# A hybrid SSD, mLSTM and RWKV-7 trunk on one core: its order from a recorded program and a list scheduler instead of hand-set yields, and GpSimd's tensor operations on VectorE

## The chip, the cores and the metric

The kernel runs on one core of a Trainium2 chip. A core has five engines with a queue of instructions each: TensorE (PE) for matmuls, with its weight loads shown apart (PEld), VectorE (DVE), ScalarE (ACT), GpSimd (POOL), and SyncE (SP), which here issues the DMAs. The engines meet by semaphores. The metric is the device time of one execution in microseconds, the median of several runs.

## The reference

The program is a trunk of two layers over 256 positions of width 1024, all in f32. A layer adds a half SwiGLU feed-forward network, then a mixer, then another half network; a last norm closes the trunk.

```python
for each layer:
    x += 0.5 * swiglu(rms_norm(x, n1), f1_gate_up, f1_down)     # 1024 -> 2 x 2816 -> 1024
    u = rms_norm(x, mix_norm) @ w_in                            # all head groups at once
    y = concat(ssd_mixer(u_ssd), mlstm_mixer(u_mlstm), rwkv7_mixer(u_rwkv))   # 1024 | 512 | 512
    x += y @ w_out                                              # 2048 -> 1024
    x += 0.5 * swiglu(rms_norm(x, n2), f2_gate_up, f2_down)
out = rms_norm(x, final_norm)
```

The three head groups are recurrences, computed in chunks:

```python
# SSD: causal convolution and silu, then in 2 chunks of 128, per head
y = (C B^T * decay) @ (X * dt) + (C @ state) * exp(a_cum) + X * d_skip
y = group_rms_norm(y * silu(z))
# mLSTM: q, k, v by small matmuls, exponential gates with a running maximum, 2 chunks of 128
# RWKV-7: per head of 64, a state that is decayed, corrected along a removal key and written to;
# in 4 chunks of 64, with a triangular inverse (I + A)^-1 per chunk and head, then a group norm
```

## The kernel before

**Precision and weights.** A large matmul is done in three passes of half precision each: weights and activations are split into a rounded `hi` and a rest `lo`, and PE adds hi·hi, hi·lo and lo·hi (L354 to L356 for projections, down and output weights, L571 to L573 for gate and up). The weights come from DRAM as 378 blocks of 128 x 1024 f32 (512 KB) through `load_next`; ACT copies each to `hi` (L327) and another engine subtracts to get `lo` (L328). That is DVE, but in the mixer every third block, from the sixth on, is subtracted on GpSimd: 18 blocks in each layer. There are six buffers of raw blocks and four of each half, and the split runs at most three blocks ahead of PE.

**Stages of a mixer.** The weight blocks are used in a fixed order: output gate, RWKV's r, k, v and low-rank inputs, the mLSTM input, the SSD input with its convolution, z, and then w_out. Beside these projections run the tasks: `rwkv` (L734 on), the gates of SSD and mLSTM, `mlstm`, and two parts of SSD. The RWKV task is one long chain: the shifted projections, tanh and decay (L748 to L800), the norm of the removal key with its matmul (L807, L808), the pair matrices of keys within a chunk (matmul L845, masked out of the bank at L850), and then an inverse of the triangular part. The 16 x 16 diagonal blocks of that matrix are written to DRAM by 16 DMAs (L887) and read back with each block on one partition (L889); 15 steps of two small DVE instructions solve all of them at once (L950, L952); the result goes out again (L959, L960) and comes back block by block (L969). From there small matmuls (L994) put the blocks together, and four chunks follow, each with some eight steps that depend on one another (L1044 to L1066). `put_yT` then transposes for w_out, which waits until RWKV has ended.

**What sets the order.** Program order is the order of each engine's queue. The tasks are Python generators that yield a number at each step; a `Driver` holds a clock which the main loop advances by hand-set amounts after each matmul group, and it resumes a task when the clock has passed what the task asked for. Where the main loop cannot go on without a task, `drv.until` runs tasks until a flag is set. The tasks' buffers come from one arena of 104 x 256 columns, and a task that finds no room yields. PSUM is split into four accumulator banks, three for projections and one for transposes.

Of the kernel before, what the change touches and what calls it, by code (L numbers as in the profile page):

```python
# [37 lines left out]
R_NM, R_SSD, R_DSK, R_ML, R_LNW, R_LNB, R_AL = 0, 1024, 2048, 3072, 3584, 4096, 4608  # L38
NPR = 4644
# [10 lines left out]
NRAW = 6  # L50
FIRST = ((0, 1), (2, 3))
FIRST_M = ((0, 1, 2, 3), ())
NHL = 4
YIELD = {'rwkv': 1.8, 'rwkv_norm': 2.07, 'gates': 1.8, 'mlstm': 1.8, 'ssd_a': 1.61, 'ssd_b': 1.8}
POOL_LO = 3
POOL_0 = 5
ADV = (10.5, 1.3, 1.3, 5.2, 2.6)
ARENA = 104 * 256


class Arena:


    def __init__(self, ap, n):
        self.ap, self.free, self.used = ap, [(0, n)], {}
        self.peak, self.n = 0, n

    def get(self, n):
        best = None
        for i, (o, m) in enumerate(self.free):  # L70
            if m >= n and (best is None or m < self.free[best][1]):
                best = i
        assert best is not None, (n, self.free)
        o, m = self.free.pop(best)
        if m > n:
            self.free.append((o + n, m - n))
        v = self.ap[:, o:o + n]
        self.used[id(v)] = (o, n, v)
        self.peak = max(self.peak, self.n - sum(m for _, m in self.free))
        return v  # L80

    def fits(self, n):
        return any(m >= n for _, m in self.free)

    def grab(self, n):

        while not self.fits(n):
            yield 1.0
        return self.get(n)

    def put(self, *views):
        for v in views:
            o, n, _ = self.used.pop(id(v))
            self.free.append((o, n))
            self.free.sort()
            merged = []
            for a, b in self.free:
                if merged and merged[-1][0] + merged[-1][1] == a:
                    merged[-1] = (merged[-1][0], merged[-1][1] + b)
                else:  # L100
                    merged.append((a, b))
            self.free = merged


class Driver:


    def __init__(self):
        self.t, self.tasks = 0.0, []

    def spawn(self, gen):
        self.tasks.append([self.t, gen])

    def _run(self, task):
        try:
            w = next(task[1])
        except StopIteration:
            self.tasks.remove(task)
            return
        task[0] = self.t + YIELD[task[1].__name__] * w  # L120

    def adv(self, dt):
        self.t += dt
        for task in list(self.tasks):
            if task[0] <= self.t:
                self._run(task)

    def until(self, ready):
        while not ready():
            task = min(self.tasks, key=lambda x: x[0])  # L130
            self.t = max(self.t, task[0])
            self._run(task)
# [3 lines left out]
def kernel(ctx: ExitStack, tc: tile.TileContext, x, pvec, prow, fnorm, w_gate,  # L136
                             w_in, w_out, f1_gu, f1_dn, f2_gu, f2_dn, wq, wk, wv, w_up, a_up, g_up, out):
    nc = tc.nc
    pe, act, dve, gps, sp = nc.tensor, nc.scalar, nc.vector, nc.gpsimd, nc.sync

    const = ctx.enter_context(tc.tile_pool(name="const", bufs=1))
    rawp = ctx.enter_context(tc.tile_pool(name="rawp", bufs=NRAW))
    hip = ctx.enter_context(tc.tile_pool(name="hip", bufs=NHL))
    lop = ctx.enter_context(tc.tile_pool(name="lop", bufs=NHL))
    rowp = ctx.enter_context(tc.tile_pool(name="rowp", bufs=1))
    smp = ctx.enter_context(tc.tile_pool(name="smp", bufs=4))
    ptp = ctx.enter_context(tc.tile_pool(name="ptp", bufs=2))
    dramp = ctx.enter_context(tc.tile_pool(name="dramp", bufs=2, space=bass.MemoryType.DRAM))
    ps_acc = ctx.enter_context(tc.tile_pool(name="ps_acc", bufs=4, space=PSUM))
    ps_mm = ctx.enter_context(tc.tile_pool(name="ps_mm", bufs=3, space=PSUM))  # L150
    ps_tr = ctx.enter_context(tc.tile_pool(name="ps_tr", bufs=1, space=PSUM))

    def mmb():
        return ps_mm.tile([128, 512], F32, tag="mm", name="mm")

    def trb():
        return ps_tr.tile([128, 512], F32, tag="tr", name="tr")

    def accb():
        return ps_acc.tile([128, 512], F32, tag="acc", name="acc")  # L160
# [7 lines left out]
    arena_t = const.tile([128, ARENA], F32, name="arena")  # L168
    ar = Arena(arena_t, ARENA)
    res = const.tile([128, 2, D], F32, name="res")  # L170
    hT_hi = const.tile([128, 8, T], F32R, name="hT_hi")
    hT_lo = const.tile([128, 8, T], F32R, name="hT_lo")
# [13 lines left out]
    br = const.tile([128, T], F32R, name="br")  # L186

# [5 lines left out]
    def build_consts():  # L193
        dve.tensor_copy(out=identr, in_=ident)
        dve.tensor_tensor(out=selr, in0=ident[:, 0:64], in1=ident[:, 64:128], op=ALU.add)
        mk = ar.get(256)
# [13 lines left out]
        bones = ar.get(128)  # L210
# [4 lines left out]
        ar.put(bones)  # L215
# [13 lines left out]
        dve.memset(mk, 0.0)  # L229
        dve.tensor_copy(out=br, in_=mk)  # L230
        ar.put(mk)
# [12 lines left out]


    specs = []
    on_pool = set()

    def spec_gu(w, j):
        for k0 in range(0, 8, 2):  # L250
# [32 lines left out]

    for l in range(DEPTH):
        spec_ffn(f1_gu[l], f1_dn[l])
        first = len(specs)
        spec_wide(w_in[l], I_O)
        for step in W_IN_ORDER:
            if step == "wag":
# [29 lines left out]
    def split_next():  # L319
# [10 lines left out]
        if n == 2:  # L330
            head.append(last.ins)
# [157 lines left out]
    def run(gen):  # L489
        for _ in gen:  # L490
            pass
# [1163 lines left out]
```

## Time and profile before

| | us |
|---|---|
| median of three runs | 1337.6 (1336.62 to 1338.77) |
| the profiled execution | 1338.6 |
| its span on the device | 1336.9 |
| mean granted TensorE clock | 0.981 of full speed |

The span runs from the first to the last instruction on the core; some 1.7 us of the execution lie outside it. Busy time of an engine is a sum over its instructions. Matmuls are pipelined, so that a matmul's own duration in a row is longer than the distance to the next. The granted clock is the mean of what the throttle gave TensorE in a window; where it reads 0.70, the same matmuls take that much longer. The names in the trace are the program's tiles: `arena` is any buffer of a task, `raw`, `hi` and `lo` are a weight block and its halves, `acc`, `mm` and `tr` are PSUM banks, `dn`, `dg` and `dh` are the DRAM copies of the 16 x 16 blocks. In the view of waits a row gives the waiting engine, tile and line, what released it, and then the total, the number of waits, and the longest one.

### The profile page before, as it was taken

The numbers are of one execution on the slowest core, as the hardware profiler recorded it, in microseconds if no ns is written. First come the engines' busy times: TensorE is split into PE (matmuls) and PEld (weight loads), VectorE is DVE, ScalarE is ACT, GpSimd is POOL, SyncE is SP. The second block draws the span as 40 slices with busy tenths as digits, with TensorE's granted clock in tenths as the row PEclk, the third lists the DMA queues.
The fourth block names the chain that finished last, engine by engine and source line by source line (L and its number), as shares of the span: only waits on it lengthen the run. The fifth ranks groups of instructions, "written<-read, shape, count | busy, mean of one in ns | idle before, by whom it ended". The sixth has DMA issues, their size and how long they took to land.

```text
span 1336.9 us, 23055 instructions
## 1 busy us (share of the span) xinstructions
PE 1273.2 (95%) x9170; PEld 1146.3 (86%) x9170; DVE 816.6 (61%) x1084; ACT 662.8 (50%) x993; POOL 224.2 (17%) x215
## 2 busy tenths in 40 slices
PE   8999999788998999999999999997899899999997
PEld 6999988788976789999989999896889677899996
DVE  6555555878557665555575555658774765655554
ACT  6444445555545564444464444464564554644443
POOL 3000002534143320000000000044511523100001
PEclk9999999889998999999999999998999989999999
DMA  9655658344423356666566666664443325556661
GB/s 293 199 184 183 190 162 222 95 119 113 149 64 95 126 175 188 186 185 184 171 189 190 186 184 185 187 178 114 104 132 99 96 66 154 188 178 187 189 189 48
DMA packets 199451, 211.38 MB, mean 158 GB/s; under 512 B 23088, under 2 KB 174512, under 8 KB 199344
## 3 DMA queue, kind: packets, MB, share of 16 engines
q1 hardware_dynamic: 199344, 209.92, 52.8%
q8 instruction: 72, 1.18, 0.4%
q14 instruction: 35, 0.29, 0.1%
HBM read 208.04 MB, written 1.84 MB: 157 GB/s over the span
## 4 chain that ended last, share of the span: by engine, by line
PE 79%; DVE 11%; ACT 3%; issue 2%; DMA 2%; POOL 1%; SPq 1%; POOLq 0%; ACTq 0%; DVEq 0%
PE mm L571 11%; PE mm L572 11%; PE mm L573 11%; PE acc L354 8%; PE acc L355 8%; PE acc L356 8%; PE mm L355 4%; PE mm L356 4%; PE mm L354 4%; DVE lo L328 2%; PE acc L994 2%; DVE arena L952 1%; PE mm L1431 1%; DVE arena L950 1%; DVE arena L704 1%
## 5 line engine op out<-in xcount | busy, mean ns | idle before, releaser
L328 DVE TENSOR_TENSOR lo<-raw,hi 128x1024 fp32r<-128x1024 f32 (+1 forms) x346 | 424.9, 1232 | 363.7 <-ACT hi L327 353.1
L327 ACT ACTIVATE hi<-raw 128x1024 fp32r<-128x1024 f32 (+1 forms) x382 | 400.7, 1052 | 445.3 <-PE mm L572 180.2
L571 PE MATMUL mm<-hT_hi,hi 128*128 128x256 f32 x1280 | 360.5, 282 | 0.0
L572 PE MATMUL mm<-hT_lo,hi 128*128 128x256 f32 x1280 | 359.5, 281 | 0.0
L573 PE MATMUL mm<-hT_hi,lo 128*128 128x256 f32 x1280 | 359.5, 281 | 0.0
L572 PEld LDWEIGHTS mm<-hT_lo,hi 128*128 128x128 f32 x1280 | 241.2, 188 | 1.8
L571 PEld LDWEIGHTS mm<-hT_hi,hi 128*128 128x128 f32 x1280 | 241.0, 188 | 1.8
L573 PEld LDWEIGHTS mm<-hT_hi,lo 128*128 128x128 f32 x1280 | 241.2, 188 | 0.0
L354 PE MATMUL mm<-hT_hi,hi 128*128 128x256 f32 x464 | 135.3, 292 | 7.9 <-DVE arena L952 3.2
L354 PE MATMUL acc<-hi,pth 128*128 128x512 f32 x352 | 139.7, 397 | 0.2
L355 PE MATMUL acc<-lo,pth 128*128 128x512 f32 x352 | 139.2, 396 | 0.0
L356 PE MATMUL acc<-hi,ptl 128*128 128x512 f32 x352 | 138.5, 395 | 0.0
L356 PE MATMUL mm<-hT_hi,lo 128*128 128x256 f32 x464 | 132.4, 285 | 0.0
L355 PE MATMUL mm<-hT_lo,hi 128*128 128x256 f32 x464 | 132.1, 285 | 0.0
L328 POOL TENSOR_TENSOR lo<-raw,hi 128x1024 fp32r<-128x1024 f32 x36 | 91.8, 2549 | 140.4 <-ACT hi L327 128.2
L390 POOL TENSOR_SCALAR ss<-ss 128x1 f32<-128x1 f32 x14 | 7.4, 528 | 568.0 <-ACT arena L386 567.8
L354 PEld LDWEIGHTS mm<-hT_hi,hi 128*128 128x128 f32 x464 | 89.2, 192 | 12.0 <-issue 9.3
L356 PEld LDWEIGHTS mm<-hT_hi,lo 128*128 128x128 f32 x464 | 89.2, 192 | 1.0 <-issue 0.6
L355 PEld LDWEIGHTS mm<-hT_lo,hi 128*128 128x128 f32 x464 | 88.9, 191 | 1.1 <-issue 0.5
L356 PEld LDWEIGHTS acc<-hi,ptl 128*128 128x128 f32 x352 | 66.0, 187 | 16.0
L354 PEld LDWEIGHTS acc<-hi,pth 128*128 128x128 f32 x352 | 66.1, 188 | 15.2 <-ACT pth L372 1.1
L355 PEld LDWEIGHTS acc<-lo,pth 128*128 128x128 f32 x352 | 66.0, 188 | 14.1
(333 smaller groups left out, 1771.0 us busy)
## 6 DMA issues: line engine op xcount, KB each, us to landing
raw<-in_f_gu_dram SPq DMA_DIRECT2D x352, 256.0 KB, 3.1
raw<-in_f_dn_dram SPq DMA_DIRECT2D x88, 512.0 KB, 3.7
raw<-in_w_in_dram SPq DMA_DIRECT2D x80, 512.0 KB, 4.2
raw<-in_w_out_dram SPq DMA_DIRECT2D x32, 512.0 KB, 3.6
arena<-in_prow_dram SPq DMA_DIRECT2D x4, 512.0 KB, 4.7
arena<-in_prow_dram SPq DMA_DIRECT2D x6, 256.0 KB, 4.7
row<-in_prow_dram SPq DMA_DIRECT2D x2, 512.0 KB, 5.1
raw<-in_w_gate_dram SPq DMA_DIRECT2D x2, 512.0 KB, 3.7
```

The source lines that it names most:

```text
L327: last = act.activation(out=hi[:, c], in_=src[:, c], func=AF.Copy)
L328: eng.tensor_tensor(out=lo[:, c], in0=src[:, c], in1=hi[:, c].bitcast(F32), op=ALU.subtract)
L354: pe.matmul(o, lhsT=ah, rhs=bh, start=start, stop=False)
L355: pe.matmul(o, lhsT=ah, rhs=bl, start=False, stop=False)
L356: pe.matmul(o, lhsT=al, rhs=bh, start=False, stop=stop)
L571: pe.matmul(o, lhsT=wh[:, k, g, b, :], rhs=hh, start=new, stop=False, skip_group_check=True)
L572: pe.matmul(o, lhsT=wh[:, k, g, b, :], rhs=hl, start=False, stop=False, skip_group_check=True)
L573: pe.matmul(o, lhsT=wl[:, k, g, b, :], rhs=hh, start=False, stop=kk == 7, skip_group_check=True)
L704: dve.scalar_tensor_tensor(out=dst[:, s:T], in0=ps[:, 0:T - s], scalar=col(cw + 3 - s), in1=dst[:, s:T], op0=ALU.mult, op1=ALU.add)
L950: dve.tensor_tensor(out=tmv[:, 0:n, 0:s + 1], in0=bc(pmv[:, s, s + 1:16, None], sh), in1=bc(gmv[:, s, None, 0:s + 1], sh), op=ALU.mult)
L952: dve.tensor_tensor(out=gmv[:, s + 1:16, 0:s + 1], in0=gmv[:, s + 1:16, 0:s + 1], in1=tmv[:, 0:n, 0:s + 1], op=ALU.subtract)
L994: pe.matmul(bv[q, n, :], lhsT=lhs(q, i * 8 + n), rhs=rhs(q, i * 8 + n), start=True, stop=True)
```

## The change

Nearly every line is touched, since each instruction is now recorded first. The engine names `pe`, `act`, `dve`, `gps`, `sp` stand for recorders; a call notes the instruction with what it reads and writes. When the whole program is recorded, `run` issues it: among the instructions whose inputs are done it picks, engine by engine, by an estimated start time and a priority, keeping a model of the engines, the DMAs, the ACT tables and the port that DVE and GpSimd share. The dense projections keep their own order. A PE instruction of a task that depends on another engine is held back by a margin in the model.

```diff
-class Driver:
-    def adv(self, dt):
...
+class Planner:
+    SEM = 60.0
+    MARGIN = 1000.0
...
+            if op.eng == "pe" and op.cross > 0:
+                t = max(t, op.cross + self.MARGIN)
...
+        def key(op, t):
+            e = op.eng
+            if e == "pe":
+                return (2, op.n) if op.dense else (op.rank, -op.tail)
+            if e == "sp":
+                return (0, op.n) if op.piece is None or op.piece < 6 else (1, op.n)
+            if op.piece is not None:
+                need = free["pe"] + (self.before[op.piece] - st["prog"])
+                return (0, op.n) if need - t < urgent[e] else (5, op.n)
+            return (op.rank, -op.tail)
...
+    with tc.manual_schedule():
+        plan.run(reserve={"f": 6144, "r": 6144}, wmin={"f": 4, "r": 4}, wmax={"f": 5, "r": 6}, urgent={"act": 7000.0, "dve": 5500.0}, keep_max=3072, spare=8)
```

Buffers are placed when their first writer is issued, in 22 regions of 2048 columns (`region` in the new program's names), for weights and tasks alike; all eight PSUM banks are one pool with caps (four accumulators, three for projections, five for tasks).

GpSimd's subtractions of the weight splits and its multiplications and additions go to DVE: GpSimd's tensor operations fall from 96 to 28 (the powers of the norms and one product of the last norm stay), DVE's rise from 715 to 785. Among them the skip term of SSD: `d_skip` comes as 16 values instead of a row of 1024, and is multiplied straight out of the PSUM bank.

```diff
-    on_pool = set()
-        on_pool.update(range(first + POOL_0, len(specs), POOL_LO))
...
-        eng = gps if n in on_pool else dve
...
-                    act.activation(out=Xv[:, t, fs], in_=b, func=AF.Copy)
-                    gps.tensor_tensor(out=Xv[:, t, fs], in0=Xv[:, t, fs], in1=drow[:, fs], op=ALU.mult)
+                    dve.tensor_tensor(out=heads(Xs[t, g]), in0=heads(b),
+                                      in1=bc(dskip[:, g * 8:g * 8 + 8][:, :, None], [128, 8, 64]), op=ALU.mult)
```

The pair matrices are held in two halves, so that the diagonal blocks leave in 32 DMAs for each mixer instead of 16:

```diff
-                        sp.dma_start(out=dnv[c, b16][:, :, h, :], in_=NMv[rows_of(c, b16), :, c, h, c0:c0 + 16])
+                        for i in range(2):
+                            sp.dma_start(out=dnv[c, b16][:, i * 4:i * 4 + 4, h, :],
+                                         in_=NMv[i][rows_of(c, b16), :, c, h, c0:c0 + 16])
```

Matmuls stay at 8346, ACT's table loads go from 13 to 10, DVE's instructions from 1084 to 1154, GpSimd's from 218 to 164, and the DMAs from 659 to 691. The order by itself, at three places:

On DVE, in the first mixer, before, the small steps of the row solve (L950, L952) stand among convolution steps (L704) and a weight split (L328):

```order
L952 TENSOR_TENSOR arena<-arena 128x4x12
L704 SCALAR_TENSOR_TENSOR arena<-mm,pv,arena 128x255
L950 TENSOR_TENSOR arena<-arena 128x3x13
L704 SCALAR_TENSOR_TENSOR arena<-mm,pv,arena 128x254
L952 TENSOR_TENSOR arena<-arena 128x3x13
L704 SCALAR_TENSOR_TENSOR arena<-mm,pv,arena 128x253
L950 TENSOR_TENSOR arena<-arena 128x2x14
L328 TENSOR_TENSOR lo<-raw,hi 128x1024
L952 TENSOR_TENSOR arena<-arena 128x2x14
L950 TENSOR_TENSOR arena<-arena 128x15
L952 TENSOR_TENSOR arena<-arena 128x15
```

There now (L1303, L1305 are the same two steps, L1134 is the convolution):

```order
L1303 TENSOR_TENSOR region_2028<-region_2028 128x8x8
L1305 TENSOR_TENSOR region_2028<-region_2028 128x8x8
L1134 SCALAR_TENSOR_TENSOR region_677<-bank_89,pv,region_677 128x255
L1134 SCALAR_TENSOR_TENSOR region_677<-bank_89,pv,region_677 128x254
L1134 SCALAR_TENSOR_TENSOR region_677<-bank_89,pv,region_677 128x253
L1303 TENSOR_TENSOR region_2028<-region_2028 128x7x9
L1305 TENSOR_TENSOR region_2028<-region_2028 128x7x9
L1303 TENSOR_TENSOR region_2028<-region_2028 128x6x10
```

The 30 steps follow one another but for these three instructions; other convolution steps and all splits stand ahead of them or behind.

On PE, in the last chunks of RWKV in the first mixer, before, every task group (L1063, L1066, L1044) has projection matmuls behind it:

```order
L1063 MATMUL acc<-arena 128x128 x4
L1066 MATMUL acc<-arena 64x64 x8
L355 MATMUL mm<-hT_lo,hi 128x256
L356 MATMUL mm<-hT_hi,lo 128x256
L354 MATMUL mm<-hT_hi,hi 128x256
L355 MATMUL mm<-hT_lo,hi 128x256
L356 MATMUL mm<-hT_hi,lo 128x256
L354 MATMUL mm<-hT_hi,hi 128x256
L355 MATMUL mm<-hT_lo,hi 128x256
L356 MATMUL mm<-hT_hi,lo 128x256
L1044 MATMUL acc<-arena 128x128 x4
L1048 MATMUL acc<-arena 64x64 x8
```

There now (L1411 to L1429 are the chunks' steps, L1584 and L1614 mLSTM's):

```order
L1426 MATMUL bank_88<-region_788,region_2911 128x128
L1429 MATMUL bank_87<-region_788,region_2368 64x64 x4
L1429 MATMUL bank_87<-region_788,region_401 64x64 x4
L1614 MATMUL bank_89<-region_1969,region_2911 128x129
L1614 MATMUL bank_88<-region_1969,region_2911 128x129
L1614 MATMUL bank_89<-region_1969,region_2911 128x129
L1614 MATMUL bank_88<-region_1969,region_2911 128x129
L1584 MATMUL bank_87<-region_677,region_2643 128x256
L1411 MATMUL bank_89<-region_3008,region_2307 128x128 x4
L1415 MATMUL bank_89<-region_2611,region_2368 64x64 x4
L1415 MATMUL bank_89<-region_2611,region_401 64x64 x4
L1584 MATMUL bank_87<-region_677,region_2643 128x256
```

The projections that stood here are now behind the chunks, and what fills the gaps is mLSTM's matmuls; between the start of the inverse and the last chunk only two weight blocks of projections are left.

On SP, around the row solve in the first mixer, before:

```order
L887 DMA dn<-arena 16x8x16 x16
L264 DMA raw<-in_w_in_dram 128x8x128
L936 DMA arena<-in_prow_dram 128x512
L889 DMA arena<-dn 128x256
L937 DMA arena<-in_prow_dram 128x512
```

There now (L1277 is the way out, in halves of half the size, L1280 the way back, L709 a weight block):

```order
L1277 DMA dn<-region_2368 16x4x16
L1277 DMA dn<-region_401 16x4x16
L709 DMA region_677<-in_w_in_dram 128x8x128
L709 DMA region_2611<-in_w_in_dram 128x8x128 x2
L709 DMA region_428<-in_w_in_dram 128x8x128
L1280 DMA region_2028<-dn 128x256
L1569 DMA region_2643<-in_wq_dram 128x4x128
```

Twice as many DMAs of half the size go out, four weight blocks are issued between the last of them and the read back, and the loads of other rows have moved.

More of the change, by code (lines that the diff above doesn't have):

```diff
@@ L105 @@
-class Driver:
[L108 to L120, printed above, removed]
-    def adv(self, dt):
[L123 to L132, printed above, removed]
+GRAIN, BLOCKS, REGIONS = 128, 16, 22
@@ new lines, with footprint @@
+MASKS = {}
+def footprint(v):
+    v = view(v)
+    row, rows = v.ap[0]
+    p0, c0 = divmod(v.offset, row)
+    key = tuple(v.ap[1:])
+    m = MASKS.get(key)
+    if m is None:
+        m = 1
+        for s, c in reversed(key):
+            if s:
+                one = m
+                for i in range(1, c):
+                    m |= one << (i * s)
+        MASKS[key] = m
+    return p0, p0 + rows, m << c0
+class Op:
+    __slots__ = ("line", "n", "eng", "call", "name", "a", "k", "bufs", "left", "succ", "ready", "cross", "occ", "dur", "table", "tail",
+                 "rank", "piece", "dense", "gate", "lock", "issued", "nbytes", "start", "wait_all")
@@ L186, with bank, mmb, accb @@
     br = const.tile([128, T], F32R, name="br")
+    smalls = const.tile([128, SLOT * SLOTS], F32, name="smalls")
+    banks = [psum.tile([128, 512], F32, name=f"bank{i}") for i in range(8)]
+    plan = Planner(nc, ctx.enter_context(tc.tile_pool(name="regions", bufs=1)), banks, smalls)
+    pe, act, dve, gps, sp = (plan.engine(n) for n in ("pe", "act", "dve", "gps", "sp"))
+    new, newr, small = plan.new, plan.newr, plan.small
+    def bank():
+        return plan.bank("task")
+    def mmb():
+        return plan.bank("main")
+    def accb():
+        return plan.bank("acc")
     def select(v, pattern, base, mult, fill, op=ALU.is_ge):
@@ L335 @@
-    AHEAD = 3
-    def weights(n=1):
-        u = state["use"]
-        while state["split"] < min(u + n, len(specs)):
-            split_next()
-        got = [ready.pop(i) for i in range(u, u + n)]
-        state["use"] = u + n
-        return got
-    def ahead(k=AHEAD):
-        while state["split"] < min(state["use"] + k, len(specs)):
-            split_next()
-    drv = Driver()
+        plan.piece = n
+        raws[n] = new(1024, "w")
+        specs[n](raws[n])
+        plan.piece = None
@@ L612, in ffn @@
                     down(j - 1, k, 1, w)
-                    ahead()
             else:
@@ L960, in rwkv @@
             sp.dma_start(out=dh.rearrange("q s t -> q (s t)"), in_=tmp)
[L961 to L964 removed]
+            G, H = (new(1024).rearrange("p (n t) -> p n t", n=16) for i in range(2))
+            gps.memset(G, 0.0, after=pm)
+            gps.memset(H, 0.0, after=pm)
             for dst, src in ((G, dg), (H, dh)):
@@ new lines, in rwkv @@
+            for n in range(0, 8, 2):
+                b = bank()
+                bv = b.rearrange("p (m c k) -> p m c k", m=2, c=2)
+                for m in range(2):
+                    for c in range(2):
+                        pe.transpose(bv[:, m, c, :], BKv[:, n + m, 2 * c:2 * c + 2, :].rearrange("p s t -> p (s t)"),
+                                     ident, after=gm)
+                act.activation(out=BT[n // 2], in_=bv, func=AF.Copy)
+            v = rkv["v"]
+            UV = [new(512) for _ in range(4)]
```

1462 lines of the change are left out of this document (808 added, 654 removed).

## The prediction

> **What bounds the kernel now.** I read the page's first part, then the span cut at its five stages, then one mixer cut at its own stages, and then what PE (TensorE) waited for.
>
> ```profile
> span 1336.9 us, 23055 instructions
> PE 1273.2 (95%) x9170; PEld 1146.3 (86%) x9170; DVE 816.6 (61%) x1084; ACT 662.8 (50%) x993; POOL 224.2 (17%) x215
> ```
>
> PE is busy for 95% of the span and the change leaves its 8346 matmuls as they are. So nothing can be won but time in which PE stands still or runs at a lower clock. Where that is, the table by stage shows (columns: window, its length, busy time of each engine, the granted clock, DMA share, GB/s); the second and fourth rows are the two mixers, the others the feed-forward halves.
>
> ```profile
> core 0: us, PE busy (x) PEld busy (x) DVE busy (x) ACT busy (x) POOL busy (x), PEclk, DMA share, GB/s
> 0.00:200.00 200.00, 192.57 (x1297) 176.28 (x1298) 113.86 (x154) 95.38 (x130) 12.13 (x39) 1.00 0.66 202
> 200.00:480.00 280.00, 255.64 (x1995) 222.66 (x1994) 189.18 (x284) 148.49 (x259) 99.54 (x75) 0.96 0.44 124
> 480.00:862.00 382.00, 381.20 (x2603) 350.95 (x2602) 218.95 (x248) 181.30 (x233) 8.48 (x15) 1.00 0.61 184
> 862.00:1141.00 279.00, 255.60 (x1994) 223.06 (x1993) 188.05 (x284) 149.30 (x261) 96.35 (x74) 0.96 0.43 121
> 1141.00:1337.00 196.00, 188.15 (x1287) 173.31 (x1285) 106.59 (x119) 88.35 (x113) 7.68 (x12) 0.99 0.54 166
> ```
>
> In the 382 us between the mixers PE is busy for 381.20 at clock 1.00: the feed-forward halves have nothing to give. A mixer takes 279.5 us (mean of 280 and 279). Its work at full clock is 255.64 x 0.96 = 245.4 us; of the other 34.1 us, 24 are idle and 10 are lost to the clock. Were all of that closed in both mixers, the kernel would gain 68 us and no more. The first mixer, cut at its stages:
>
> ```profile
> 201.00:285.00 84.00, 72.33 (x519) 65.24 (x517) 62.47 (x86) 42.44 (x70) 32.12 (x23) 0.92 0.56 150
> 285.00:330.00 45.00, 39.63 (x318) 37.83 (x318) 38.64 (x78) 30.08 (x51) 20.75 (x19) 1.00 0.48 121
> 330.00:384.00 54.00, 53.88 (x729) 49.08 (x729) 24.07 (x46) 27.47 (x45) 5.92 (x5) 1.00 0.32 96
> 384.00:480.00 96.00, 88.80 (x427) 69.72 (x426) 63.00 (x75) 48.01 (x95) 40.74 (x29) 0.95 0.37 116
> ```
>
> These are the front (projections, gates, the RWKV pair matrices), the row solve of those matrices through DRAM, their inverse with the four chunks, and the SSD part with w_out. Idle: 11.7, 5.4, 0.1 and 7.2 us. Clock: 72.33 x 0.08 = 5.8 in the front and 4.4 in the back. What PE waits for (total, times, longest, over both mixers):
>
> ```profile
> PE acc L807 <- ACT pth L372: 11.0, 2, 5.7
> PE acc L1161 <- DVE arena L1156: 6.5, 2, 3.7
> PE acc L1308 <- DVE arena L1387: 5.3, 2, 2.7
> PE mm L354 <- DVE arena L952: 3.2, 2, 2.9
> PE mm L354 <- DVE arena L950: 2.9, 1, 2.9
> ```
>
> Each is a task's matmul, or a weight block queued behind one, waiting for a chain of ACT and DVE steps, with no other PE work placed ahead of it.
>
> **Part 1: PE's order.** I count PE's work in the new order at measured pitches. A 128x256 matmul takes (226.25 - 215.01) / 95 = 0.118 us, by the first and last of 96 in a row; the pair multiplications take 10.4 / 319 per pass, from the group below.
>
> ```profile
> 215.01 0.28 PE L354 MATMUL mm<-hT_hi,hi 128*128 128x256 f32 x1
> 226.25 0.28 PE L356 MATMUL mm<-hT_hi,lo 128*128 128x256 f32 x1
> ...
> L994 PE MATMUL acc<-arena 64*64 64x64 f32 x319 | 10.4, 219 | 0.1
> ```
>
> Ahead of the inverse stood 72.33 x 0.92 + 39.63 = 106 us at full clock; now 91 us do, and 15 us of projections have gone behind the chunks.
>
> *Front.* Ahead of the row-norm matmul (L807, now L1209) stood 7.6 us of weight blocks and now 12.9, which covers 5.3 of its 5.5 us of wait. The gate matmuls (L1161, now L1504) have 4.5 us ahead and 6.0 behind where they waited 3.25. So I leave 4 us of the 11.7, mostly single steps between a transpose and its reader; bounds 0 and 11.7.
>
> *Row solve.* The rows of its chain:
>
> ```profile
> 285.31 8.37 SPq L887 DMA_DIRECT2D dn<-arena  x16
> 295.09 0.34 SPq L889 DMA_DIRECT2D arena<-dn  x1
> 299.44 0.17 DVE L950 TENSOR_TENSOR arena<-arena 128x15 f32<-128x15 f32 x1
> 322.33 0.34 SPq L959 DMA_DIRECT2D dg<-arena  x1
> 324.08 3.75 SPq L969 DMA_DIRECT2D arena<-dg  x8
> 329.76 2.43 PE L994 MATMUL acc<-arena 64*64 64x64 f32 x64 [0.66 <-DMA arena<-dg]
> ```
>
> It took 329.76 - 285.31 = 44.5 us. The largest piece is the loop of 30 small DVE instructions, 322.33 - 299.44 = 22.9 us, because splits and convolution steps stood between them and because GpSimd stretched them:
>
> ```profile
> L952 DVE TENSOR_TENSOR arena<-arena 128x15 f32<-128x15 f32 (+7 forms) x15 | 8.0, 533 | 0.3
> L950 DVE TENSOR_TENSOR arena<-arena 128x15 f32<-128x15 f32 (+7 forms) x15 | 7.3, 488 | 0.2
> L952 DVE TENSOR_TENSOR arena<-arena x30: 175/222/2395, 299.6 to 981.2; 128x15 f32<-128x15 f32 x4, 128x28 f32<-128x28 f32 x4, 128x39 f32<-128x39 f32 x4, 128x48 f32<-128x48 f32 x4
> L704 DVE SCALAR_TENSOR_TENSOR arena<-mm,pv,arena 128x255 f32<-128x255 f32 (+2 forms) x42 | 20.0, 479 | 12.0 <-ACT arena L702 11.4
> ```
>
> The new order puts three convolution steps and no split between them. At the median of 0.222 that is 30 x 0.22 + 3 x 0.479 = 8.0 us; at the stretched means 15.3 + 1.4 = 16.7. Against that, the matrices now leave in 32 DMAs instead of 16; some 26 are issued after the last eviction, at 8.37 / 16 = 0.52 each 13.5 us, with four weight issues behind them on SP (1.6). The sum: 13.5 + 1.6 + 0.3 + 4.35 (landing, 295.09 to 299.44) + 8.0 + 1.75 (322.33 to 324.08) + 5.7 (324.08 to 329.76) = 35.2 us. Behind the last pair-matrix matmul stand 39.6 us of PE work in the new order, so nothing is idle here; at the stretched means the chain is 44 and 4 us are.
>
> *Inverse and chunks.* In that window are 85 projections of 256 columns and 30 of 512 (85 x 0.118 + 30 x 0.233 = 17 us), so the tasks were 37. The new order keeps 4 us of projections and brings 4 of other tasks: 45 us of PE work, with almost nothing to fill a wait. Bounds: 45, no idle, and before's pace of 54, 9 idle. A chunk's steps depend on one another and each needs an eviction, so I stay nearer the slow end: 6 us. This is a new wait, and it takes back a quarter of the gain.
>
> *Back.* The 15 us come here. DVE needs for each block one split (of the size of L790, below) and three convolution steps, 1.23 + 3 x 0.479 = 2.67 us, and PE 24 x 0.118 = 2.83: DVE just keeps pace. I leave 3 us of 7.2; bounds 0 and 7.2.
>
> **Part 2: GpSimd's work on DVE.** The rows (GpSimd over both mixers, DVE in the first):
>
> ```profile
> L328 POOL TENSOR_TENSOR lo<-raw,hi 128x1024 fp32r<-128x1024 f32 x36 | 91.8, 2549 | 140.4 <-ACT hi L327 128.2 <-PE acc L748 12.2
> L1390 POOL TENSOR_TENSOR arena<-arena 128x512 f32<-128x512 f32 x8 | 12.3, 1537 | 5.8 <-ACT arena L1386 5.8
> L328 DVE TENSOR_TENSOR lo<-raw,hi 128x1024 fp32r<-128x1024 f32 x39 | 51.0, 1313 | 29.5 <-ACT hi L327 27.0 <-DMA raw<-in_w_out_dram 2.5
> L800 DVE TENSOR_TENSOR arena<-arena 128x1024 f32<-128x1024 f32 x1 | 3.3, 3257 | 0.0
> L790 DVE TENSOR_TENSOR arena<-arena 128x1024 f32<-128x1024 f32 x1 | 1.2, 1226 | 2.3 <-ACT arena L774 2.3
> ```
>
> DVE gains 18 splits, at the 1.23 us of L790 22 us in each mixer and some 13 us of smaller operations (the four L1390, now L1697 out of the bank, 2.7). It gets back what overlap with GpSimd cost it: the same form took 3257 ns in L800 and 1226 in L790, and the small loop 15.3 us instead of 6.6; over a mixer I put this at 30 us (0 to 30). So DVE goes from 189 to between 194 and 224 us of some 264: room enough on average. I cost part 2 at nothing beyond the above; its cover is that DVE's queue is short where the chain runs, and what it costs without that cover is the second rival.
>
> **Clock.** I take the loss in proportion to the idle time: idle 4 + 0 + 6 + 3 = 13 of 24.4, so 10.2 x 13 / 24.4 = 5.4 us; bounds 0 and 10.2. What comes ahead of a low clock:
>
> ```profile
> 240.00:250.00 10.00, 6.97 (x59) 6.76 (x58) 7.66 (x8) 4.74 (x6) 3.94 (x4) 0.96 0.40 105
> 250.00:260.00 10.00, 7.31 (x45) 6.97 (x46) 8.54 (x9) 5.62 (x9) 2.79 (x2) 0.70 0.41 107
> 400.00:410.00 10.00, 6.83 (x39) 5.61 (x38) 9.68 (x8) 6.88 (x11) 5.78 (x3) 0.98 0.33 91
> 410.00:420.00 10.00, 10.00 (x46) 6.76 (x46) 5.26 (x14) 7.08 (x21) 0.00 (x0) 0.85 0.39 119
> ```
>
> Windows with 3.0 and 3.2 us of idle are followed by clocks of 0.70 and 0.85. (The Trainium skill, "TensorE: Matmul & The Clock Gate", section "Why this matters for your kernels", says that the clock falls only after a gap of more than about 3 us; these rows agree with it. By that rule 13 us in short gaps would lose nothing: the third rival.)
>
> **Sum.** A mixer takes 245.4 + 13 + 5.4 = 263.8 us, 15.7 less than 279.5. The profiled execution took 1338.6 us, 1.0 over the median of 1337.6: 1338.6 - 2 x 15.7 - 1.0 = 1306 us.
>
> **Rivals.**
> 1. *The RWKV chain is not shortened (slower).* Up to the last chunk PE has 91 + 45 = 136 us of work now and had 160, and it got there in 384 - 201.7 = 182 us. If only the row solve's 9 us come off, the chain is 173; PE idles 37 us there and 3 behind, the clock loses its 10, and a mixer takes 295.4: 1338.6 + 31.8 - 1.0 = 1369 us. It decides from 136 + (34.1 - 3 - 10) = 157 us on; I expect some 148. For it: the old order filled these waits with the very projections that are now late. Against it: PE was busy 72 of the front's 84 us, so it was mostly the projections ahead of the chain that made the front long.
> 2. *DVE becomes the limit (no change).* The stretch is not GpSimd's doing and stays; the loop costs 4.5 us idle, and of the 18 splits, at 1.313 = 23.6 us, half come in front of chain steps. A mixer takes 263.8 + 16.3 = 280: 1339 us. For it: DVE works 62 of 84 us in the front already. Against it: L800 against L790.
> 3. *No gap reaches the length that lowers the clock.* Then the 5.4 us go: 1338.6 - 2 x 21.1 - 1.0 = 1295 us. For it, the four windows; against it, that a chain may still leave one gap of 3 us in each mixer.
>
> **How the numbers follow.** Forecast 0.55, rival 1 0.17, rival 2 0.16, rival 3 0.12. The bounds alone give 247.4 (idle 2, no loss: 1273 us) to 279.5 (1338 us); the range leaves out the low corner and the longer half of rival 1: 1282 to 1350. A measurement tells 0.2% from no change (2.7 us). Faster: 0.55 + 0.12 + half of rival 2, 0.75; slower: rival 1 and a part of rival 2, 0.20; the same, 0.05.
>
> **What would show it.** Right: PE's count unchanged, mixer windows near 264 us, L807's and L1161's waits gone, the small loop in some 8 us, new waits in the chunks of 6 us, the two-buffer forms of DVE near 1.23 us. Wrong: over 20 us of idle ahead of the last chunk (rival 1), DVE busy for over 220 us in a mixer with PE waiting for splits (rival 2), feed-forward windows that are no longer full, or clock 1.00 in both mixers (rival 3).

## The result, and the profile after

The new kernel takes 1302.85 us (median of four runs, 1300.19 to 1305.16) against 1337.97 us before in the same comparison (1336.62 to 1338.77): a ratio of 0.9738, with a 95% interval of 0.9717 to 0.9758. The forecast was 1306. The profiled execution took 1305.16 us, the slowest of the four.

The page's first part, columns as before:

```profile
span 1303.4 us, 22885 instructions
PE 1263.1 (97%) x9170; PEld 1150.5 (88%) x9170; DVE 807.2 (62%) x1154; ACT 643.4 (49%) x993; POOL 86.1 (7%) x161
```

PE has the same 9170 matmuls by the page's count (no row here shows the 8346 named earlier) and is idle for 40.3 us instead of 63.7. GpSimd is down from 224 to 86 us, and DVE, with 70 instructions more, is busy for 9 us less. The table by stage:

```profile
0.00:200.00 200.00, 192.60 (x1296) 177.63 (x1296) 113.53 (x155) 95.68 (x133) 9.94 (x36) 1.00 0.72 229
200.00:464.00 264.00, 251.72 (x2005) 223.56 (x2006) 191.24 (x324) 147.29 (x264) 30.38 (x49) 0.98 0.42 124
464.00:846.00 382.00, 379.06 (x2590) 351.42 (x2589) 212.40 (x243) 172.58 (x232) 10.09 (x17) 1.00 0.60 187
846.00:1109.00 263.00, 253.19 (x2003) 224.44 (x2004) 189.04 (x322) 146.81 (x259) 28.25 (x48) 0.98 0.41 121
1109.00:1303.00 194.00, 186.58 (x1280) 173.44 (x1278) 101.00 (x114) 81.07 (x109) 7.47 (x12) 0.99 0.44 146
```

The mixers take 264 and 263 us where they took 280 and 279; the 382 us of feed-forward work between them are unchanged. The first mixer, cut at the same points of the program as before (start of the mixer, first DMA of the diagonal blocks, inverse, last chunk):

```profile
201.00:262.00 61.00, 59.06 (x426) 52.48 (x427) 48.37 (x59) 34.95 (x54) 9.80 (x16) 0.97 0.29 77
262.00:311.00 49.00, 42.46 (x330) 40.12 (x326) 35.55 (x98) 31.13 (x73) 7.01 (x17) 0.93 0.43 97
311.00:361.50 50.50, 48.24 (x685) 44.12 (x684) 29.87 (x56) 29.62 (x62) 1.86 (x2) 1.00 0.23 70
361.50:464.00 102.50, 101.95 (x575) 86.84 (x574) 76.44 (x113) 50.58 (x75) 11.30 (x14) 1.00 0.58 191
```

The front has shrunk from 84 to 61 us and the back has grown from 96 to 102.5, since projections have moved behind the chunks. Idle: 1.9, 6.5, 2.3 and 0.6 us. PE's longest waits over the whole span (the second row is the wait for x at the head of the program, the third stands at the start of each mixer, the others are in the mixers):

```profile
PE bank L1575 <- DVE region L1543: 7.4, 2, 4.6
PE bank L870 <- DMA res<-in_x_dram: 4.8, 1, 4.8
PE bank L865 <- DVE region L918: 3.4, 2, 1.8
PE bank L1504 <- DVE region L1124: 3.1, 2, 1.6
PE bank L1165 <- ACT region L1169: 2.1, 4, 0.6
```

The row norm's wait (11.0) has gone from the list, and the gates' (L1504) is 3.1 instead of 6.5. The longest is new: the value matmul of mLSTM (L1575). The timeline shows where it comes from:

```profile
288.89 0.23 PE L1540 MATMUL bank<-ident,t 68*128 68x68 f32 x1
299.74 0.38 DVE L1307 COPY region<-region 128x256 f32<-128x256 f32 x1
300.03 0.16 DVE L1541 COPY region<-bank 128x8 f32<-128x8 f32 x1
300.11 0.15 DVE L1543 TENSOR_TENSOR region<-bank,region 128x8 f32<-128x8 f32 x1
300.31 0.94 PE L1575 MATMUL bank<-region,region 128*128 128x128 f32 x6 [2.78 <-DVE region L1543]
```

A transpose of the gates ends at 289; the two small instructions that read its bank (L1541, L1543) stand on DVE behind the 30-step solve and its copy, which end at 300; and L1575 follows at once. It needs nothing that they write (its operands are the mLSTM input and `wqkv_v`), so what it waits for must be the bank.

The solve on DVE, and its chain:

```profile
L1305 DVE TENSOR_TENSOR region<-region 128x15 f32<-128x15 f32 (+7 forms) x15 | 3.1, 207 | 0.5
L1303 DVE TENSOR_TENSOR region<-region 128x15 f32<-128x15 f32 (+7 forms) x15 | 3.1, 206 | 0.4
...
262.37 15.71 SPq L1277 DMA_DIRECT2D dn<-region  x32
282.03 1.59 SPq L1280 DMA_DIRECT2D region<-dn  x1
291.19 0.17 DVE L1303 TENSOR_TENSOR region<-region 128x15 f32<-128x15 f32 x1
299.77 0.34 SPq L1310 DMA_DIRECT2D dg<-region  x1
311.10 2.26 PE L1369 MATMUL bank<-region,region 64*64 64x64 f32 x64
```

The steps take 206 ns on average where they took 488 and 533, and the loop 8.6 us with its three convolution steps, where it took 22.9. The chain as a whole is no shorter: the inverse starts at 311, 48.7 us after the first DMA.

### The profile page after: what moved, and what is told of

It reads as the page before. It is cut to its first block, busy times and chain, and to the rows that moved or that the text cites. A ratio compares the mean times of both kernels' runs of the same rounds, so it can differ in the third digit from the quotient of the medians.

```text
span 1303.4 us, 22885 instructions
## 1 busy us (share of the span) xinstructions
PE 1263.1 (97%) x9170; PEld 1150.5 (88%) x9170; DVE 807.2 (62%) x1154; ACT 643.4 (49%) x993; POOL 86.1 (7%) x161
## 3 DMA queue, kind: packets, MB, share of 16 engines
HBM read 207.01 MB, written 1.84 MB: 160 GB/s over the span
## 4 chain that ended last, share of the span: by engine, by line
PE 87%; DVE 7%; ACT 3%; issue 1%; SPq 1%; DMA 1%; POOLq 0%; DVEq 0%; POOL 0%; ACTq 0%
PE bank L806 25%; PE bank L808 25%; PE bank L807 25%; PE bank L1369 2%; DVE region L774 1%; SPq L1277 1%; PE bank L1727 1%; ACT region L773 1%; DVE region L1243 1%; PE bank L1420 1%; DVE region L1134 1%; PE bank L1415 1%; PE bank L1429 1%; PE bank L870 1%; PE bank L1584 1%
## 5 line engine op out<-in xcount | busy, mean ns | idle before, releaser
L806 PE MATMUL bank<-region,region 128*128 128x256 f32 (+1 forms) x2384 | 749.5, 315 | 2.3 <-DVE region L1243 0.9
L807 PE MATMUL bank<-region,region 128*128 128x256 f32 (+1 forms) x2384 | 748.3, 314 | 0.0
L808 PE MATMUL bank<-region,region 128*128 128x256 f32 (+1 forms) x2384 | 747.8, 314 | 0.3 <-DVE region L825 0.3
L806 PEld LDWEIGHTS bank<-region,region 128*128 128x128 f32 x2384 | 456.6, 192 | 30.8 <-DVE region L1243 1.3
L808 PEld LDWEIGHTS bank<-region,region 128*128 128x128 f32 x2384 | 456.9, 192 | 28.0 <-issue 1.5
L807 PEld LDWEIGHTS bank<-region,region 128*128 128x128 f32 x2384 | 456.7, 192 | 27.9 <-issue 2.9
L774 DVE TENSOR_TENSOR region<-region,region 128x1024 fp32r<-128x1024 f32 (+1 forms) x382 | 443.8, 1207 | 23.7 <-ACT region L773 22.7
L773 ACT ACTIVATE region<-region 128x1024 fp32r<-128x1024 f32 (+1 forms) x382 | 375.1, 1039 | 17.6 <-ACT region L773 8.4
L1025 DVE TENSOR_TENSOR region<-bank,region 128x512 f32<-128x512 f32 (+1 forms) x44 | 27.9, 642 | 269.2 <-PE bank L808 269.1
L1026 ACT ACTIVATE region<-region 128x512 f32<-128x512 f32 (+1 forms) x44 | 25.7, 593 | 329.6 <-DVE region L1025 329.6
L1134 DVE SCALAR_TENSOR_TENSOR region<-bank,pv,region 128x255 f32<-128x255 f32 (+2 forms) x84 | 39.9, 480 | 27.0 <-ACT region L1132 23.6
L824 ACT ACTIVATE region<-region 128x512 fp32r<-128x512 f32 (+1 forms) x48 | 28.1, 596 | 43.0 <-DVE region L1027 42.8
L825 DVE TENSOR_TENSOR region<-region,region 128x512 fp32r<-128x512 f32 (+1 forms) x48 | 30.5, 646 | 25.8 <-ACT region L824 25.8
L1027 DVE TENSOR_TENSOR region<-bank,region 128x512 f32<-128x512 f32 (+1 forms) x44 | 27.6, 635 | 0.2 <-ACT region L1026 0.2
L1557 ACT ACTIVATE region<-bank,region 128x128 f32<-128x128 f32 x80 | 23.4, 378 | 5.8 <-PE bank L1553 3.0
```

What stands on the lines that cost most here:

```text
L773: act.activation(out=hi[:, c], in_=src[:, c], func=AF.Copy)
L774: dve.tensor_tensor(out=lo[:, c], in0=src[:, c], in1=hi[:, c].bitcast(F32), op=ALU.subtract)
L806: pe.matmul(o, lhsT=ah, rhs=bh, start=start, stop=False, skip_group_check=True)
L807: pe.matmul(o, lhsT=ah, rhs=bl, start=False, stop=False, skip_group_check=True)
L808: pe.matmul(o, lhsT=al, rhs=bh, start=False, stop=stop, skip_group_check=True)
L824: act.activation(out=hi, in_=src, func=AF.Copy)
```

## The experiments

The prediction left one thing open that the total can't tell: whether the gain is the order (part 1) or GpSimd's work (part 2). **Theory: the order. Rival: GpSimd's work taken away.** Five kernels were meant to take one without the other. None of them holds the order still. In the kernels with the new planner, an edit changes the planner's input, so that it also sets other instructions otherwise. In the old kernel PE's order changes too, although the edits there only swap engine names and the `Driver`'s hand-set clock does not see engines: counted in the traces from the first mixer's first transpose on, 417 projection matmuls (L354 to L356) stand ahead of its gates (L1161) in the old kernel, and 491 in the one with everything on DVE. So the old queues are not simply the program order, as the section on the kernel before has it. The time of each kernel is therefore that of its work and of the order that came with it.

**The new kernel with the splits back on GpSimd.**

```diff
-                dve.tensor_tensor(out=lo[:, c], in0=src[:, c], in1=hi[:, c].bitcast(F32), op=ALU.subtract)
+                (gps if u in on_pool else dve).tensor_tensor(out=lo[:, c], in0=src[:, c], in1=hi[:, c].bitcast(F32), op=ALU.subtract)
```

> The new kernel, but every third weight split of the mixer goes back to GpSimd (18 in each layer). If the gain is the order of PE (theory), the time stays near the new kernel, 1300 to 1312 us: the splits take about 2.5 us each on GpSimd, and the 30-step solve on DVE becomes slower than its 8.3 us, but PE has other work in that time. If the gain is GpSimd's work taken away (rival), most of it is lost: 1315 to 1338 us, with DVE instructions stretched to over 2 us and new PE waits for DVE.

Measured: 1308.69 us, ratio to the old kernel 0.9783 (0.9766 to 0.9799), within the theory's range. The group of splits in the first mixer:

```profile
L777 DVE TENSOR_TENSOR region<-region,region 128x1024 fp32r<-128x1024 f32 x37 | 56.8, 1557 | 3.4 <-ACT region L776 3.3
```

DVE's splits are stretched to 1557 ns, more than in the old kernel (1313), and yet PE's idle time is only 4 us over the new kernel's (44.1). The planner answered with another order: from the start of the inverse to the last chunk step of the first mixer stand 177 projection matmuls, where the new kernel has 34 and the old one 115. That they cover a late DVE fits this, but is not shown by itself.

**The old kernel with all of it on DVE.**

```diff
-        eng = gps if n in on_pool else dve
+        eng = dve
...
-            gps.tensor_tensor(out=BKv[:, :, 0::3, :], in0=pair(k), in1=pair(mPi), op=ALU.mult)
+            dve.tensor_tensor(out=BKv[:, :, 0::3, :], in0=pair(k), in1=pair(mPi), op=ALU.mult)
```

> The old kernel with its old order, but all weight splits and the eight other tensor operations of the mixer's tasks that stood on GpSimd on DVE. If the order is the gain (theory), the waits of PE that the order causes (for the row norm, for the gates) stay, and the time is 1328 to 1345 us. If GpSimd's work taken away is the gain (rival), it falls to 1300 to 1322 us. Either way the small steps of the solve should show no duration over 0.3 us if GpSimd is what stretched them.

Measured: 1309.43 us, 0.9792 (0.9777 to 0.9806): the time is in the rival's range, and the theory's was missed by 19 us. Without the new planner 28 of the 35 us are gained. The mixers, two of PE's longest waits, the group of splits (its second number is the mean in ns), and the source view of the two steps of the solve (shortest, median and longest in ns, then the first and last start; L952 in both mixers, L950 in the first):

```profile
200.00:466.00 266.00, 252.74 (x2002) 219.85 (x2002) 187.57 (x322) 150.79 (x263) 25.62 (x41) 0.98 0.46 131
848.00:1112.00 264.00, 250.87 (x1990) 218.20 (x1989) 184.58 (x318) 148.71 (x258) 23.13 (x40) 0.97 0.44 126
...
PE acc L1237 <- ACT arena L701: 7.8, 4, 2.6
PE acc L1199 <- ACT t L1193: 6.6, 2, 3.3
...
L328 DVE TENSOR_TENSOR lo<-raw,hi 128x1024 fp32r<-128x1024 f32 (+1 forms) x382 | 461.6, 1212 | 363.0 <-ACT hi L327 353.0 <-DMA raw<-in_f_gu_dram 3.3 <-DMA raw<-in_f_dn_dram 3.1
...
L952 DVE TENSOR_TENSOR arena<-arena x30: 168/201/222, 301.8 to 966.6; 128x15 f32<-128x15 f32 x4, 128x28 f32<-128x28 f32 x4, 128x39 f32<-128x39 f32 x4, 128x48 f32<-128x48 f32 x4
...
L950 DVE TENSOR_TENSOR arena<-arena x15: 166/200/221, 300.7 to 320.7; 128x15 f32<-128x15 f32 x2, 128x28 f32<-128x28 f32 x2, 128x39 f32<-128x39 f32 x2, 128x48 f32<-128x48 f32 x2
```

The waits at L807 (11.0), L1161 (6.5) and L1308 (5.3) are gone from the head of the list, and others have grown: L1199 had 1.9 us before. That DVE's chains end sooner is one reason, the changed order the other: the gates' matmul (L1161) starts 2.4 us earlier, but behind 74 more projection matmuls, some 8.7 us of PE work at 0.118 us each. No step of the solve takes over 222 ns, where one took 2395. Yet the first and the last of the L950 steps start 20.0 us apart, where it was 22.5 in the old kernel: the loop stays long, since six splits and 18 convolution steps now stand among its steps, where there were three and twelve, and the inverse starts later (334.6 us, 329.8 before). The gain is not the solve. DVE is busy for 810.7 us in all, less than before (816.6), with 68 instructions more. The splits among these are 36 at 1.212 us, 44 us, so that overlap with GpSimd had cost DVE some 50 us, and more by what the 32 others take. The old kernel's own trace agrees: the 16 of the 60 solve steps that overlap a GpSimd instruction on tensors took 1.35 us on average, the other 44 took 0.2.

**Which part of GpSimd's work?** Two old kernels, one with only the splits moved, one with only the nine other operations.

> The old kernel with only the weight splits moved from GpSimd to DVE. They are 92 of GpSimd's 224 us and the longest single instructions beside DVE's; if the overlap with them is what slows the chain (theory), most of the 28 us that moving everything gave come from here: 1310 to 1320 us. If the chain's own operations on GpSimd matter more (rival), 1322 to 1337 us.

> The old kernel with only the nine other tensor operations of the mixer's tasks moved to DVE and the splits left on GpSimd. By the theory of the splits: 1326 to 1337 us. By the rival: 1310 to 1322 us.

Measured: 1312.70 us with the splits moved (0.9815, 0.9801 to 0.9830), 1310.82 us with the tasks' operations moved (0.9811, 0.9790 to 0.9832). Both expectations named one part as the cause, and both were wrong as such: either part brings nearly all of it, 25 and 27 us, and both together 28. Of the wait at L807, 6.9 us are left with the tasks' operations moved and 3.9 with the splits moved. The start of that matmul in the first mixer (the two times behind the durations), in the old kernel, with the splits moved, and with the tasks' operations moved:

```profile
L807 PE MATMUL acc<-pth,bonesr x2: 628/712/795, 252.7 to 253.7; 128*128 128x512 f32 x2
...
L807 PE MATMUL acc<-pth,bonesr x2: 444/474/504, 252.8 to 253.3; 128*128 128x512 f32 x2
...
L807 PE MATMUL acc<-pth,bonesr x2: 628/712/796, 250.8 to 251.9; 128*128 128x512 f32 x2
```

With the splits moved it starts no earlier: the wait shrank because 314 projection matmuls stand ahead of it instead of 293. With the tasks' operations moved the 293 are unchanged and it starts 1.9 us earlier: there the chain is shorter.

**The new planner with nearly all of it on GpSimd.** The first experiment, and seven of the eight other operations:

```diff
-            dve.tensor_tensor(out=pair(r), in0=ARv[:, :, 0::3, :], in1=BKv[:, :, 0::3, :], op=ALU.mult)
+            gps.tensor_tensor(out=pair(r), in0=ARv[:, :, 0::3, :], in1=BKv[:, :, 0::3, :], op=ALU.mult)
...
-                dve.tensor_tensor(out=bonv[:, t], in0=bonv[:, t], in1=lnb, op=ALU.add)
+                gps.tensor_tensor(out=bonv[:, t], in0=bonv[:, t], in1=lnb, op=ALU.add)
```

> The new kernel with the 18 splits and seven of the eight other operations of a mixer back on GpSimd (one multiplication, at L1224, stays on DVE, and the skip term is as in the new kernel): the new order almost alone. If order and GpSimd's work are two ways to the same gain (theory: each removes PE's waits for the DVE chain, one by putting work in front, the other by shortening the chain), it loses little more than the splits alone, 1308 to 1316 us. If the smaller operations are what hurts, being in the RWKV chain itself (rival), 1318 to 1338 us.

Measured: 1316.49 us, 0.9842 (0.9828 to 0.9857), half a microsecond above the theory's range and below the rival's. All of it together (idle is the span less PE's busy time; low windows are the stretches of 3.41 us at half clock in the trace's clock record, each of which costs 1.7 us; both from the profiled execution; the last column counts the projection matmuls from the start of the first mixer's inverse to the last chunk step):

| kernel | weight splits | other operations | us | PE idle | low windows | projections |
|---|---|---|---|---|---|---|
| old | GpSimd | GpSimd | 1337.6 | 63.7 | 13 | 115 |
| old | GpSimd | DVE | 1310.8 | 42.3 | 10 | 75 |
| old | DVE | GpSimd | 1312.7 | 48.1 | 6 | 75 |
| old | DVE | DVE | 1309.4 | 42.5 | 7 | 59 |
| new planner | GpSimd | GpSimd (7 of 8) | 1316.5 | 49.1 | 8 | 110 |
| new planner | GpSimd | DVE | 1308.7 | 44.1 | 6 | 177 |
| new planner | DVE | DVE | 1302.85 | 40.3 | 6 | 34 |

The new planner with GpSimd's work brings 21 us, that work moved in the old kernel 28, both 35 and not 49. Both draw on one stock of idle time: a shorter DVE chain, or other work in front of the matmuls that wait for it. How much of the 28 us is the one and how much the other stays open, since the last column moves in every row: no run changes the work at a fixed order.

**The planner's margin.** `MARGIN = 1000.0` becomes `MARGIN = 0.0`.

> The new kernel with the planner's margin for task matmuls that depend on another engine set from 1000 to 0. If the margin is what keeps projections in front of tasks that are not ready (theory), PE waits more in the front and the chunks: 1306 to 1325 us. If the planner's durations are good enough without it (rival), 1299 to 1305 us.

Measured: 1306.32 us (0.9758 to 0.9787 of the old). That is at the lower edge of the theory's range and only 3.5 us over the new kernel, with intervals that touch: the margin is worth little here.

**The gate copies ahead of the solve.** First the whole gate task, ranked ahead of the others; then only its last transposes and the two copies behind them.

```diff
-            task()
+            with ranked(1 if i == 0 else 2):
+                task()
```

> The new kernel with the gate task ranked ahead of the other tasks, so that its last two small DVE copies (L1541, L1543) stand ahead of the 30-step solve instead of behind it. If PE's wait of 2.8 to 4.6 us at the mLSTM value matmul (L1575) comes from that place in DVE's queue (theory), the wait goes, with the low clock behind it: 1292 to 1299 us. If the RWKV chain decides there anyway (rival), PE waits as long at the first inverse matmul (L1369) instead: 1300 to 1306 us.

> The new kernel with only the last four gate instructions (two transposes, two DVE copies out of their bank) ranked ahead, where ranking the whole gate task put the pair matrices late. If PE's wait at L1575 is the place of these copies behind the 30-step solve (theory), the wait of 4.6 and 2.8 us goes and with it one or two windows of low clock, 1292 to 1299 us; if the first inverse matmul (L1369) then waits instead (rival), 1300 to 1305 us.

Measured: 1312.99 us (0.9806 to 0.9837) for the whole task, worse by 10 and outside both expectations; PE then waits 5.3 us at the pair matrices (L1238) and the clock is low in ten windows: from 257.1 to 263.0 DVE's queue serves gate steps and a split, and the first copy of the pair matrices (L1243) starts at 263.0 instead of 260.5. With only the last instructions ranked: 1302.61 us (0.9730 to 0.9773), the same as the new kernel. Its waits:

```profile
PE bank L1504 <- DVE region L1124: 3.2, 2, 1.6
PE bank L1339 <- ACT region L1329: 2.0, 2, 1.7
...
PE bank L1576 <- DVE region L1134: 1.9, 1, 1.9
...
PE bank L1327 <- ACT region L1341: 1.3, 2, 0.6
PE bank L1369 <- ACT region L1329: 1.2, 1, 1.2
PE bank L1369 <- ACT region L1378: 1.1, 1, 1.1
```

The 7.4 us at the value matmul (now L1576) are down to 1.9, so the place in DVE's queue was their cause. But new waits of 1 to 2 us stand at the next task matmuls, PE's idle time is 40.6 us as before (40.3), and the median does not move. The rival expected as long a wait at the inverse (L1369): 2.3 us of the new waits stand there, the rest one step earlier.

**The diagonal blocks through two queues.**

```diff
-                            sp.dma_start(out=dnv[c, b16][:, i * 4:i * 4 + 4, h, :],
+                            (gps if h else sp).dma_start(out=dnv[c, b16][:, i * 4:i * 4 + 4, h, :],
```

> The new kernel with half of the 32 DMAs that carry the diagonal blocks to DRAM issued by GpSimd's queue instead of SP's. They take 15.7 us on SP, so that the solve ends up to 7 us earlier. If PE's work behind the pair matrices covers the solve (theory: PE waited 0.7 us for it), nothing is gained: 1300 to 1306 us. If the solve is on the path (rival), the time falls by 3 to 10 us: 1293 to 1300 us.

Measured: 1298.80 us, 0.9709 (0.9695 to 0.9722), 4 us under the new kernel, as the rival said; all four runs (1297.41 to 1299.59) lie under the new kernel's four.

```profile
261.77 8.61 SPq L1281 DMA_DIRECT2D dn<-region  x16
273.58 0.34 SPq L1284 DMA_DIRECT2D region<-dn  x1
283.57 0.34 SPq L1314 DMA_DIRECT2D dg<-region  x1
...
262.66 8.34 POOL L1281 DMA_DIRECT2D dn<-region  x16 [8.22 <-DVE region L1247]
```

The 32 DMAs are out by 271 instead of 278, and the solve is done 16 us earlier (283.6 instead of 299.8). The second queue is 7 us of that. The rest came with the planner's new order: one weight load instead of four is issued ahead of the read back, which then lands in 2.1 us (6.1 in the new kernel), and the first step starts 2.2 us behind its issue instead of 9.2. The gate copies no longer stand behind it, PE's idle time falls from 40.3 to 36.6 us and the low windows from 6 to 2. That PE waited only 0.7 us at the inverse did not show that the solve was free: what it held up was queued behind it on DVE.

**Work without use in PE's gaps.** Clock records of the first ten kernels suggested that a window of 3.41 us with about half of it idle is enough for half clock in the next one. Twelve matmuls without use fill the 1.7 us at each mixer's start, and 16 transposes the head of the program:

```diff
+                    for _ in range(FILL):
+                        pe.matmul(b[:, 0:256], lhsT=identr, rhs=maskr.rearrange("p c l -> p (c l)"),
+                                  start=True, stop=True, after=last)
```

> The new kernel, in which PE does 12 matmuls of 256 columns without use at the start of each mixer, while it waits 1.7 us for the mixer's first transposes, and 16 transposes without use at the head of the program while it waits for x. Nothing else in the order changes. If a window of 3.4 us in which PE is idle for about half or more is what halves the clock in the next window (theory, from the clock records of all runs so far), the low windows at 202.6 us and at the second mixer's start go, and the first projections run at full clock: 3 to 5 us less than the new kernel, 1298 to 1300 us. If only gaps of over 3 us do that (rival), these two low windows have another cause and stay: 1302 to 1304 us.

> The fill matmuls together with the four ranked gate instructions, as the candidate for the fastest kernel. If the two are independent (theory), 1297 to 1300 us; if the fill does nothing (rival), 1300 to 1304 us.

> The kernel with the blocks' DMAs on two queues (1298.8 us) and the 12 matmuls without use at each mixer's start, without those at the head; engine by engine the order is that of the former but for these matmuls. Its two wait rows at the mixers' start are 3.5 us together, and no low window followed them in its profile. If a window of half idle time decides by where the free-running windows fall (theory), the fill gives little here, on average 0 to 2 us, and less scatter: 1296 to 1299 us. If the matmuls in front of the transposes delay them (rival), 1299 to 1302 us.

Measured: 1302.05 us (0.9719 to 0.9746) on the new kernel, within the rival's range; 1297.71 us (0.9688 to 0.9714) with the ranked copies, within the theory's, where the copies alone had 1302.61; 1299.30 us (0.9703 to 0.9739) with two queues, 0.3 us into the rival's, where the queues alone had 1298.80. In windows of 3.4 us, the first mixer's start in the new kernel, and then with the fill:

```profile
199.17:202.58 3.41, 1.69 (x10) 1.01 (x10) 3.41 (x5) 2.64 (x7) 1.18 (x2) 1.00 1.01 278
202.58:205.99 3.41, 3.41 (x8) 2.25 (x9) 3.41 (x6) 0.43 (x1) 0.91 (x2) 0.50 0.60 162
205.99:209.40 3.41, 3.41 (x20) 2.87 (x20) 1.35 (x3) 1.20 (x2) 0.00 (x0) 1.00 0.83 211
```

```profile
198.20:201.60 3.40, 3.40 (x22) 3.02 (x20) 3.07 (x5) 3.28 (x6) 0.98 (x3) 1.00 0.62 166
201.60:205.00 3.40, 2.79 (x15) 1.62 (x13) 3.40 (x6) 1.73 (x4) 2.05 (x3) 1.00 0.54 145
205.00:208.40 3.40, 3.40 (x20) 2.87 (x19) 2.50 (x4) 0.63 (x2) 0.00 (x0) 1.00 0.82 212
```

In the new kernel PE is busy for 1.69 of 3.41 us, and the next window has clock 0.50, in which the 512-column matmuls start 0.43 us apart where it is 0.23 at full clock. With the fill that window is gone. But in the second mixer the low window, some 20 us behind its start, stayed, another one came up at that place in the first, and the head gained nothing: the first mixer's transposes start at 202.0 us instead of 201.1. In all, the low windows fell from 6 to 4. A gain of the fill by itself is not shown: -0.8, -4.9 and +0.5 us on three kernels. The two fastest kernels are the one with fill and ranked copies, 1297.7, and the one with two queues, 1298.8; their intervals overlap.

## Why the prediction was right, and where it was not

**The time and the mixers: right.** 263.8 us were forecast for a mixer, 264 and 263 came; 1306 us in all, 1302.85 came.

**Idle time: the sum right, the places wrong.** I left 4, 0, 6 and 3 us in front, row solve, chunks and back; it was 1.9, 6.5, 2.3 and 0.6. That errors of 2 to 6.5 us cancel to 11.3 against 13 is luck. The chunks did not stay near before's pace; the bound of "45, no idle" was the nearer one.

**The row solve: the loop right, the chain mis-sized.** The loop's 8.0 us came as 8.6. The terms around it were too small: 15.8 us for the DMAs out instead of 13.5; 3.8 us for the four weight issues instead of 1.6; 9.2 us from the read back to the first step instead of 4.35, of which 6.1 went until its data had landed, and at the end of which DVE was busy with a split and convolution steps; and 11.3 us from the last step to the inverse instead of 7.5. The chain took 48.7 us, not 35.2. "Nothing is idle here" failed not at the inverse, where PE waited for 0.7 us, but by a wait that I had not seen: a bank held by copies behind the late solve, 2.8 us in this mixer. Another 1.6 us are the gates' wait, which I had counted in the front.

**The clock: the size right, the rule not shown.** 5.4 us per mixer were forecast; 251.72 x 0.02 = 5.0 came, three low windows in each mixer. But the loss does not follow the idle time: kernels with 39.5 us (no margin), 40.3 (new) and 40.6 (ranked copies) of idle time had 4, 6 and 3 low windows.

**Part 2 at nothing: the step that failed.** I put GpSimd's work at no gain of its own beyond the shorter loop, and let the order carry the sum. Moving that work brings the old kernel 28 us, and putting it back costs the new one 14 (1316.5 less 1302.85), each with the order that came with it. The 30 us of stretched DVE time in a mixer were in the prediction; it drew from them only the loop, and without any stretch the old kernel's loop is but 2.5 us shorter, with more other work among its steps. For the other chains that PE waits for it drew nothing; one of them, up to the row norm, ends 1.9 us earlier with the tasks' operations on DVE. DVE's balance was nearly right: 191 and 189 us in the mixers, where the low end was 194.

**The rivals.** The chain did get shorter ahead of the last chunk, so that the slower case did not come: PE was there after 160 us instead of 182, with 10.7 us idle, where this rival needed over 20. DVE is not the limit (191 us, few waits for splits). The third rival, that no gap reaches the length that lowers the clock, failed: PE's waits in the mixers of the new kernel are under 3 us but for one of 4.6, yet low windows stayed in both. The Trainium skill ("TensorE: Matmul & The Clock Gate", section "Why this matters for your kernels") gives gaps of over about 3 us as the condition. The runs say otherwise, and so does one of the two rows that the prediction read as agreeing: ahead of the clock of 0.85 stands a single gap of 2.7 us (the wait at L1308), not 3.2.

What stays open is how the 35 us divide between the order and GpSimd's work, and why in the old kernel either half of that work was enough to bring nearly the whole gain. In both halves PE's order changed alike (75 projection matmuls behind the inverse, where there were 115), so that the order may be what they share; no run tests it.

## What to carry to other kernels

An order that hides a late chain and an edit that shortens the chain draw on the same idle time: do not add them up, since here 21 and 28 us made 35. Where something sets the order from the program, an edit of one instruction moves others: before a run is called the test of one cause, count what stands ahead of the waits in both traces. An instruction on a second engine is to be priced with what it does to the first: with 68 more instructions DVE was busy for less time than beside GpSimd. A wait of 0.7 us at the end of a chain does not show that the chain is free; look at what is queued behind it on its engine.

## What the runs showed of the hardware

- In the profiles of the 14 kernels, every one of the 43 windows of 3.41 us in which PE was idle for 1.84 us or more was followed by a window at half clock; of those with 1.2 to 1.84 us idle, 17 of 56 were (the head and the end of the program left out). In each trace the low stretches start whole multiples of 3.413 us apart, so that the windows run on their own, and the same gap costs 1.7 us or nothing, depending on where they fall. The new kernel's two mixers show it: at the start of the first a gap of 1.69 us lies in one window and a low window follows; at the start of the second a gap of 1.75 us is cut by a window's edge (1.55 and 0.2 us), and none follows. With the ranked copies it is the other way round. That fits the wider scatter of the new kernel's runs (5 us against 2), which was not tested by itself.
- Overlap with GpSimd cost DVE some 50 us of busy time or more in the old kernel, and instructions of 0.2 us took up to 2.4.
- A small DMA (4 KB) costs GpSimd's queue somewhat more than SP's: 0.51 us each against 0.42, at the median. For 16 of them 8.34 and 8.61 us passed, one on SP having taken 1.64.
